# Joining two matmuls of 256 columns into one of 512 in three of the seven Strassen products of a SwiGLU gate/up pair

## The chip, the cores and the metric

The kernel runs on one core of one Trainium2 chip. The metric is device time in microseconds (us) of one execution. Differences between kernels are told against the kernel before on the same chip.

The core has five engines with a queue of instructions each: TensorE (PE, matrix products into PSUM; its weight loads are listed as PEld), VectorE (DVE), ScalarE (ACT), GpSimd (POOL), and SyncE (SP, which here only issues loads). Each engine works through its own queue in order, and waits on semaphores where an operand comes from another engine or a buffer is still in use.

## What is computed

Two layers of an encoder block on x of 512 tokens by 1024 features, in float32:

```python
for l in range(2):
    x = x + 0.5 * swiglu(rms_norm(x, ffn1_norm[l]), w_gate1[l], w_up1[l], w_down1[l])
    h = rms_norm(x, mix_norm[l])
    p = h @ w_in[l]
    ...                       # attention on one part of p, a convolution on the other
    x = x + concat([attn, conv]) @ w_out[l]
    x = x + 0.5 * swiglu(rms_norm(x, ffn2_norm[l]), w_gate2[l], w_up2[l], w_down2[l])
    x = rms_norm(x, post_norm[l])

def swiglu(x, w_gate, w_up, w_down):          # 1024 -> 2816 -> 1024
    return (silu(x @ w_gate) * (x @ w_up)) @ w_down
```

The change lies in swiglu, which runs four times (two in each layer; "FFN 1" to "FFN 4" below, in order of time).

## The kernel before

**Split operands.** A float32 operand is held as two tiles: hi, the value rounded to the type that TensorE multiplies (fp32r), and lo, the rest. ACT makes hi with a copy, DVE makes lo with a subtraction. A product is three matmuls into the same PSUM area (`mm3`, lines 151 to 155): weight hi by activation hi (L152), weight hi by activation lo (L153), weight lo by activation hi (L154).

**Chunks and pairs.** The 2816 hidden features are 11 pairs of 2 x 128 (a pair is gate and up of 256 hidden features). `CHUNKS` (line 39) groups the pairs of an FFN as (0,1), (2,3,4), (5,6,7), (8,9,10). The loop is in `ffn_body`, lines 491 to 573.

- Chunk 0 is done with plain products of 512 tokens. In its second half the generator `operands` (lines 304 to 346) makes the activation operands for all later pairs, in steps that `advance` doles out between the plain work: from four quarters of the scaled x it forms the seven Strassen operands b11, b21, b22, t1 to t4 and splits each with `halved` (lines 306 to 312), 14 times in an FFN: one ACT copy of 128x512 (L310) and one DVE subtraction of 128x512 (L311), which give one hi tile and one lo tile that each hold two 256-token blocks. Behind it comes a plain down projection of 8 blocks: for each block the weight is split (L136 on ACT, L142 on DVE), multiplied, and added to x by DVE (L558).
- Every pair of chunks 1 to 3 (`pair`, lines 377 to 428; 9 in an FFN, 36 in all) is one level of Strassen-Winograd: 7 products instead of 8, on weight quarters of 128x1024 that hold gate and up side by side. `product` (lines 348 to 357) does one of them in 24 matmuls of 256 columns: 4 blocks of k, three matmuls each, for gate and for up. Gate lies in the first, up in the second half of one PSUM bank.
- Chunks 1 and 2 end with `down` (lines 430 to 477), the down projection as Strassen products, two column groups g of seven products each; a product has 6 `mm3`, so 18 matmuls of 256 columns. Chunk 3 ends with a plain down projection.

**Order inside a pair.** The products run in the order b11, b21, t2, t3, t1, t4, b22. Accumulation is in three PSUM banks: bx takes b11, t2, t1 and b22; by takes b21; bz takes t3 and t4. Between them the partial sums are copied out by ACT (`copied`, L360) or added by DVE: L389 adds by, L400 forms the difference of bz and bx after t1, L402 adds bz after t4, L408 and L409 read bx after b22. silu is L391, L405 and L408, the product with up L392, L406 and L409. The weight sums for the next pair are four DVE additions of 128x1024 (L385 to L388), which may start only after L400 of the pair before (`order["first"]`). ACT makes the hi of a weight sum (L242, L374) and DVE its lo (L244); for b21 and t4 the lo comes through a POOL DMA that adds (`subtracted`, L366 and L367). The last pair before a `down` is followed there by L460, L461 and L465 in place of L386 to L388 (weights of 128x768), and in `down` each finished product is added into x by DVE straight from PSUM (L449), ahead of the next product that accumulates in the same bank.

**What sets the order.** The queues of the engines are not written by hand: the program is built with a scheduler that orders each engine's instructions by its own estimates, under the dependencies and the hints `tc.issue_after`. PE takes all products in program order. Weight buffers hold four hi tiles and four lo tiles (`bufs=4`), PSUM has a pool of seven banks, and short-lived tiles come from a pool of five (`tmp`).

Of the kernel before, what the change touches and what calls it, by code (L numbers as in the profile page):

```python
# [15 lines left out]
P = 128  # L16
D = 1024
S = 512
# [37 lines left out]
WOP = 4  # L56
EVP = "DAD"
ORDER = "t0s1p3v4o5"

VECS = [("g1", 8), ("gm", 8), ("g2", 8), ("gp", 8), ("gql", 3), ("gkl", 2),  # L60
        ("cw", 4 * CK), ("cb", 4), ("lg", 4), ("lb", 4), ("gq", 1), ("gk", 1)]
# [11 lines left out]
def encoder_kernel(ctx: ExitStack, tc: tile.TileContext, xT, consts, vecs, rgain, wgu1, wd1, wdq1,  # L73
# [177 lines left out]
    def ffn_body(fpool, l, gx, norm, wgu, wd, wdq, gain, done, w0, halved):  # L251
# [52 lines left out]
        def operands(R):  # L304

            def halved(src, own=False):
                hi, lo = (fpool.tile([P, S], FR, tag="xs", name=nm("xs"), bufs=2) if own else slot(FR)
                          for _ in range(2))
                h3, l3 = (v.rearrange("p (j t) -> p j t", j=2) for v in (hi, lo))
                A.copy(h3, src)  # L310
                V.tensor_tensor(l3, src, h3.bitcast(FP), ALU.subtract)  # L311
                return hi, lo

            def diff(a, b, op=ALU.subtract):
                t = tmp().rearrange("p (j t) -> p j t", j=2)
                V.tensor_tensor(t, a, b, op)
                return t
            for i in range(2):
                e, o = wide(quarter()), wide(quarter())
                for j in range(2):  # L320
                    for par, t in ((0, e), (1, o)):
                        m = 4 * i + 2 * j + par
                        V.scalar_tensor_tensor(t[:, j], x[:, m, :], gain[:, m:m + 1], R, ALU.mult, ALU.mult)
                        yield
                b11, b12, b21, b22 = (v[:, :, h * HS:(h + 1) * HS] for v in (e, o) for h in range(2))
                for n, src in (("b11", b11), ("b21", b21)):
                    X[n].append(halved(src))
# [5 lines left out]
                X["t2"].append(halved(t2))  # L333
                yield
                X["t3"].append(halved(t3))
                yield
                t1 = diff(b11, b12)
                yield
                X["t1"].append(halved(t1))
                yield  # L340
                t4 = diff(b21, t2, ALU.add)
                yield
                X["t4"].append(halved(t4))
                yield
                X["b22"].append(halved(b22, i == 1))
                yield

        def product(o, w, n, start, stop):
            with tc.issue_after(order["pe"]):
                for gu in range(2):  # L350
                    for k in range(4):
                        hi, lo = X[n][k // 2]
                        t = slice(k % 2 * HS, (k % 2 + 1) * HS)
                        c = slice(gu * 512 + k * P, gu * 512 + (k + 1) * P)
                        last = mm3(o[:, gu * HS:(gu + 1) * HS], w[0][:, c], w[1][:, c], hi[:, t], lo[:, t],
                                   start and gu == 0 and k == 0, stop and k == 3, True)
            order["pe"] = last

        def copied(o, src):
            A.copy(o, src)  # L360
            return o

        def subtracted(w, src, n=WC):

# [12 lines left out]
        def pair(p, quartered):  # L377

            a11, a12, a21, a22, s3 = quarters(wgu[l, p], WC, p == CHUNKS[0][1])
            bx, by, bz = bank(), bank(), bank()  # L380
            product(bx, split_into("a11", a11), "b11", True, True)
            a = copied(tmp(), bx)
            product(by, summed(wgu[l, p, 1], a12), "b21", True, True)
            with after("first"):
                V.tensor_tensor(s3, a11, a21, ALU.add)  # L385
                V.tensor_tensor(a21, a21, a22, ALU.add)  # L386
                V.tensor_tensor(a11, a11, a21, ALU.add)  # L387
                V.tensor_tensor(a12, a12, a11, ALU.add)  # L388
# [11 lines left out]
            order["first"] = V.tensor_tensor(r2[:, 1], d, r2[:, 1], ALU.subtract).ins  # L400
            product(bz, summed(wgu[l, p, 3], a22), "t4", False, True)
            V.tensor_tensor(r2[:, 0], bz, r2[:, 0], ALU.subtract)  # L402
# [3 lines left out]
            V.tensor_tensor(s2v, s2v, r2[:, :, HS:S], ALU.mult)  # L406
            product(bx, split_into("s4", a12), "b22", False, True)
            A.activation(s[:, HS:S], bx[:, 0:HS], AF.Silu)  # L408
            V.tensor_tensor(s[:, HS:S], s[:, HS:S], bx[:, HS:S], ALU.mult)  # L409
# [8 lines left out]
            V.tensor_tensor(u[:, h0], s[:, h1], s2[:, h1], ALU.subtract)  # L418
            order["u0"] = V.tensor_tensor(u[:, h1], u[:, h0], s[:, h0], ALU.subtract).ins
            V.tensor_tensor(v[:, h0], s[:, h0], s[:, h1], ALU.subtract)  # L420
            V.tensor_tensor(v[:, h1], s2[:, h0], u[:, h1], ALU.add)
# [785 lines left out]
```

## Time and profile before

| what | before |
|---|---|
| median of 3 runs | 1806.97 us (1805.7 to 1807.44) |
| profiled execution, span of the core | 1803.8 us |
| profiled execution, mean granted TensorE clock | 0.999 |
| matmuls on PE in the trace | 12198 |
| POOL busy | 422.2 us, 23% of the span |
| DMA moved | 226.23 MB, mean 125 GB/s |

The span runs from the first to the last instruction of the profiled execution; the profile gives no other time of that execution, and the median of the runs lies 3.2 us above the span. A row of a timeline has the start in us from the span's beginning, the duration in us, the engine, the line of the kernel, the operation, output and inputs by their names in the program, their shapes, and in brackets how long the engine had been idle before and what released it. Matmuls are pipelined: consecutive ones overlap, so what one costs is the step from its start to the next start, not its duration.

### The profile page before, as it was taken

What the parts mean: (1) busy time and instruction counts of PE and PEld (TensorE: products, weight loads), DVE (VectorE), ACT (ScalarE), POOL (GpSimd) and SP (SyncE); (2) the same over time, 40 slices, a digit from 0 to 9 for tenths busy, and PEclk for the clock granted to TensorE, in tenths of its full rate; (3) what the DMA queues carried; (4) which work ended last, traced back from release to release, by engine and by line L of the source; (5) the groups of instructions that cost most, each with busy time, mean ns of one, the idle gap of its engine ahead of it and who ended that gap; (6) DMA issues with size and microseconds to landing.
All of it is one profiled execution on the core that took longest, in us unless ns stands there. A gap on an engine that the chain in (4) does not pass through costs nothing.

```text
span 1803.8 us, 30598 instructions
## 1 busy us (share of the span) xinstructions
PE 1786.7 (99%) x12198; PEld 1645.8 (91%) x12198; DVE 1423.3 (79%) x1975; ACT 1088.8 (60%) x1685; POOL 422.2 (23%) x343
## 2 busy tenths in 40 slices
PE   9999999999999999999999999999999999999998
PEld 7899999888788899999888999998978788999997
DVE  7888887588956979887779888866999668888873
ACT  5565656457953565656635656554779535656564
POOL 1000000258843000000310000002589410000001
PEclk9999999999999999999999999999999999999999
DMA  5657574324102466664326575743250126575742
GB/s 172 165 132 193 123 187 112 108 88 135 31 24 99 126 163 162 151 163 126 123 65 170 122 195 121 194 110 110 80 147 6 52 79 167 129 189 126 187 112 73
DMA packets 70415, 226.23 MB, mean 125 GB/s; under 512 B 7936, under 2 KB 8320, under 8 KB 70272
## 3 DMA queue, kind: packets, MB, share of 16 engines
q1 hardware_dynamic: 54000, 169.74, 28.1%
q0 software_dynamic: 16128, 54.53, 17.7%
q8 instruction: 95, 1.56, 0.4%
q14 instruction: 48, 0.39, 0.1%
q10 hardware_dynamic: 144, 0.00, 0.0%
HBM read 222.15 MB, written 2.10 MB: 124 GB/s over the span
## 4 chain that ended last, share of the span: by engine, by line
PE 80%; DVE 8%; ACT 5%; POOL 3%; issue 3%; DMA 1%; SPq 0%; ACTq 0%; POOLq 0%; DVEq 0%
PE ps L154 26%; PE ps L152 25%; PE ps L153 25%; POOL y L896 2%; PE ps L834 1%; DVE wl L244 1%; ACT pr L892 1%; DVE x L449 1%; DVE r L160 1%; ACT r L806 1%; PE ps L800 1%; DVE wl L142 1%; DVE cv L888 1%; DMA raw<-in_wgu 1%; ACT wh L136 1%
## 5 line engine op out<-in xcount | busy, mean ns | idle before, releaser
L153 PE MATMUL ps<-r,wh 128*128 128x256 f32 (+1 forms) x3436 | 1062.3, 309 | 0.1
L152 PE MATMUL ps<-r,wh 128*128 128x256 f32 (+1 forms) x3436 | 1061.0, 311 | 0.6 <-ACT r L159 0.3
L154 PE MATMUL ps<-r,wl 128*128 128x256 f32 (+1 forms) x2668 | 845.6, 318 | 2.6 <-DVE wl L142 1.2
L152 PEld LDWEIGHTS ps<-r,wh 128*128 128x128 f32 x3436 | 650.9, 190 | 38.6 <-ACT wh L136 2.1
L153 PEld LDWEIGHTS ps<-r,wh 128*128 128x128 f32 x3436 | 652.3, 190 | 36.4 <-issue 2.4
L154 PEld LDWEIGHTS ps<-r,wl 128*128 128x128 f32 x2668 | 506.9, 190 | 41.3 <-DVE wl L142 3.0
L136 ACT CAST wh<-raw 128x1024 fp32r<-128x1024 f32 (+3 forms) x148 | 132.1, 900 | 211.0 <-issue 101.3
L367 POOL DMA_DIRECT2D ls<-in_wgu x72 | 62.5, 869 | 741.7 <-ACT ls L366 615.3
L242 ACT CAST wh<-fr 128x1024 fp32r<-128x1024 f32 (+1 forms) x160 | 157.6, 985 | 101.5 <-DVE fr L387 39.7
L142 DVE TENSOR_TENSOR wl<-raw,wh 128x1024 fp32r<-128x1024 f32 (+3 forms) x132 | 146.8, 1117 | 91.0 <-ACT wh L136 90.0
L154 PE MATMUL ps<-r,ls 128*128 128x256 f32 x768 | 216.7, 282 | 0.0
L244 DVE TENSOR_TENSOR wl<-fr,wh 128x1024 fp32r<-128x1024 f32 (+1 forms) x160 | 182.9, 1143 | 40.3 <-ACT wh L242 40.3
L896 POOL TENSOR_TENSOR y<-y,pr 128x511 f32<-128x511 f32 (+14 forms) x120 | 157.4, 1312 | 54.6 <-ACT pr L892 47.4
L154 PEld LDWEIGHTS ps<-r,ls 128*128 128x128 f32 x768 | 145.2, 189 | 0.0
L244 DVE TENSOR_TENSOR wl<-raw,wh 128x1024 fp32r<-128x1024 f32 (+1 forms) x100 | 113.7, 1137 | 24.6 <-ACT wh L242 24.1
L189 POOL TENSOR_TENSOR r<-r,t 128x512 f32<-128x512 f32 x45 | 77.4, 1728 | 172.7 <-ACT t L185 171.9
L242 ACT CAST wh<-raw 128x1024 fp32r<-128x1024 f32 (+1 forms) x100 | 97.9, 979 | 27.9 <-PE ps L153 19.9
L366 ACT ACTIVATE ls<-fr 128x1024 fp32r<-128x1024 f32 (+1 forms) x56 | 56.1, 1002 | 78.6 <-PE ps L154 65.2
L892 ACT ACTIVATE pr<-r,vec 128x511 f32<-128x511 f32 (+14 forms) x120 | 85.3, 735 | 10.1 <-POOL y L896 10.1
L888 DVE SCALAR_TENSOR_TENSOR cv<-r,vec,cv 128x511 f32<-128x511 f32 (+14 forms) x120 | 88.0, 733 | 3.4 <-ACT cv L884 2.1
L449 DVE SCALAR_TENSOR_TENSOR x<-ps,x 128x512 f32<-128x512 f32 x112 | 77.1, 689 | 15.8 <-PE ps L154 15.4
L367 POOL DMA_DIRECT2D ls<-in_wdq x32 | 27.6, 863 | 260.5 <-ACT ls L366 260.5
(220 smaller groups left out, 2441.5 us busy)
## 6 DMA issues: line engine op xcount, KB each, us to landing
fr<-in_wgu SPq DMA_DIRECT2D x112, 512.0 KB, 3.4
ls<-in_wgu POOLq DMA_DIRECT2D x72, 512.0 KB, 6.3
raw<-in_wgu SPq DMA_DIRECT2D x62, 512.0 KB, 5.0
fr<-in_wdq SPq DMA_DIRECT2D x48, 384.0 KB, 4.6
ls<-in_wdq POOLq DMA_DIRECT2D x32, 384.0 KB, 4.7
raw<-in_wd SPq DMA_DIRECT2D x32, 384.0 KB, 3.1
raw<-in_wd SPq DMA_DIRECT2D x32, 256.0 KB, 2.7
raw<-in_wcv SPq DMA_DIRECT2D x16, 512.0 KB, 3.2
```

The lines of the kernel that those rows point to most:

```text
L136: order["cast"] = A.copy(hi[:, :w], raw[:, :w]).ins
L142: (G if kind in POOLW.split() else V).tensor_tensor(lo[:, :w], raw[:, :w], hi[:, :w].bitcast(FP), ALU.subtract)
L152: T.matmul(o, lh, rh, start=first, stop=False, skip_group_check=free)
L153: T.matmul(o, lh, rl, start=False, stop=False, skip_group_check=free)
L154: order["mm"] = T.matmul(o, ll, rh, start=False, stop=last, skip_group_check=free).ins
L242: A.copy(hi[:, :w], src[:, :w])
L244: order["lo"] = V.tensor_tensor(lo[:, :w], src[:, :w], hi[:, :w].bitcast(FP), ALU.subtract).ins
L367: G.dma_start(out=lo[:, :n], in_=w, accum_op=ALU.add)
L449: return V.scalar_tensor_tensor(v, o.rearrange("p (m t) -> p m t", m=2), 0.5 * sign, v, ALU.mult, ALU.add).ins
L888: V.scalar_tensor_tensor(acc[:, s:], u[c][:, :S - s], tap(k), acc[:, s:], ALU.mult, ALU.add)
L892: A.activation(pr[:, s:], u[c][:, :S - s], AF.Copy, scale=tap(k))
L896: order["conv"] = G.tensor_tensor(acc[:, s:], acc[:, s:], pr[:, s:], ALU.add).ins
```

## The change

In the products b21, t4 and b22 the two matmuls that share a weight tile, hi by hi and hi by lo, become one matmul of 512 columns. For that, hi and lo of an activation block have to lie side by side, and so do the two results:

- `halved` makes, for each of the two 256-token blocks, one tile with hi in the first and lo in the second half. It issues two ACT copies and two DVE subtractions of 128x256 in place of one each of 128x512, for all seven operands.
- Each of bx, by and bz becomes two banks, one for gate and one for up (six banks in place of three). A joined product leaves hi by hi plus lo by hi in the first half of each bank (the main part), and hi by lo in the second half (the rest).
- `product` issues 16 matmuls for the three joined names (8 of 512 and 8 of 256 columns) and 24 of 256 as before for b11, t2, t3 and t1.
- `copied` is two ACT copies of 128x256. Where by and bz are read, DVE adds main and rest of both halves in four instructions of 128x256 in place of one of 128x512. After b22 both halves are first copied out by ACT into a new short-lived tile y, DVE adds the rest in two instructions, and silu and the product with up read y and no longer PSUM.

`down`, the plain products and the attention and convolution part have no edit.

```diff
+JOINED = ("b21", "t4", "b22")
...
             def halved(src, own=False):
-                hi, lo = (fpool.tile([P, S], FR, tag="xs", name=nm("xs"), bufs=2) if own else slot(FR)
-                          for _ in range(2))
-                h3, l3 = (v.rearrange("p (j t) -> p j t", j=2) for v in (hi, lo))
-                A.copy(h3, src)
-                V.tensor_tensor(l3, src, h3.bitcast(FP), ALU.subtract)
-                return hi, lo
+                made = []
+                for j in range(2):
+                    both = fpool.tile([P, S], FR, tag="xs", name=nm("xs"), bufs=2) if own else slot(FR)
+                    A.copy(both[:, 0:HS], src[:, j])
+                    V.tensor_tensor(both[:, HS:S], src[:, j], both[:, 0:HS].bitcast(FP), ALU.subtract)
+                    made.append(both)
+                return made
...
-        def product(o, w, n, start, stop):
+        def product(os, w, n, start, stop):
             with tc.issue_after(order["pe"]):
-                for gu in range(2):
+                for gu, o in enumerate(os):
                     for k in range(4):
-                        hi, lo = X[n][k // 2]
-                        t = slice(k % 2 * HS, (k % 2 + 1) * HS)
+                        both = X[n][k]
                         c = slice(gu * 512 + k * P, gu * 512 + (k + 1) * P)
-                        last = mm3(o[:, gu * HS:(gu + 1) * HS], w[0][:, c], w[1][:, c], hi[:, t], lo[:, t],
-                                   start and gu == 0 and k == 0, stop and k == 3, True)
+                        first, end = start and k == 0, stop and k == 3
+                        if n in JOINED:
+                            T.matmul(o, w[0][:, c], both, start=first, stop=False, skip_group_check=True)
+                            last = T.matmul(o[:, 0:HS], w[1][:, c], both[:, 0:HS], start=False, stop=end,
+                                            skip_group_check=True).ins
+                        else:
+                            last = mm3(o[:, 0:HS], w[0][:, c], w[1][:, c], both[:, 0:HS], both[:, HS:S],
+                                       first, end, True)
             order["pe"] = last
 
-        def copied(o, src):
-            A.copy(o, src)
+        def copied(o, os):
+            for gu in range(2):
+                A.copy(o[:, gu * HS:(gu + 1) * HS], os[gu][:, 0:HS])
             return o
+
+        def parts(os):
+            return [(slice(gu * HS, (gu + 1) * HS), o[:, 0:HS], o[:, HS:S]) for gu, o in enumerate(os)]
...
-            bx, by, bz = bank(), bank(), bank()
+            bx, by, bz = ((bank(), bank()) for _ in range(3))
...
-            V.tensor_tensor(a, a, by, ALU.add)
             s = tmp()
-            A.activation(s[:, 0:HS], a[:, 0:HS], AF.Silu)
+            for c, main, rest in parts(by):
+                V.tensor_tensor(a[:, c], a[:, c], main, ALU.add)
+                V.tensor_tensor(a[:, c], a[:, c], rest, ALU.add)
+                if c.start == 0:
+                    A.activation(s[:, 0:HS], a[:, 0:HS], AF.Silu)
...
-            V.tensor_tensor(r2[:, 0], bz, r2[:, 0], ALU.subtract)
+            for c, main, rest in parts(bz):
+                V.tensor_tensor(r2[:, 0, c], main, r2[:, 0, c], ALU.subtract)
+                V.tensor_tensor(r2[:, 0, c], rest, r2[:, 0, c], ALU.add)
...
-            A.activation(s[:, HS:S], bx[:, 0:HS], AF.Silu)
-            V.tensor_tensor(s[:, HS:S], s[:, HS:S], bx[:, HS:S], ALU.mult)
+            y = copied(tmp(), bx)
+            for c, main, rest in parts(bx):
+                V.tensor_tensor(y[:, c], y[:, c], rest, ALU.add)
+                if c.start == 0:
+                    A.activation(s[:, HS:S], y[:, c], AF.Silu)
+            V.tensor_tensor(s[:, HS:S], s[:, HS:S], y[:, HS:S], ALU.mult)
```

More of the change, by code (lines that the diff above doesn't have):

```diff
@@ L326, in operands @@
                 for n, src in (("b11", b11), ("b21", b21)):
-                    X[n].append(halved(src))
+                    X[n].extend(halved(src))
                     yield
@@ L332, in operands @@
                 yield
-                X["t2"].append(halved(t2))
+                X["t2"].extend(halved(t2))
                 yield
-                X["t3"].append(halved(t3))
+                X["t3"].extend(halved(t3))
                 yield
@@ L338, in operands @@
                 yield
-                X["t1"].append(halved(t1))
+                X["t1"].extend(halved(t1))
                 yield
@@ L342, in operands @@
                 yield
-                X["t4"].append(halved(t4))
+                X["t4"].extend(halved(t4))
                 yield
-                X["b22"].append(halved(b22, i == 1))
+                X["b22"].extend(halved(b22, i == 1))
                 yield
-        def product(o, w, n, start, stop):
+        def product(os, w, n, start, stop):
             with tc.issue_after(order["pe"]):
-                for gu in range(2):
+                for gu, o in enumerate(os):
                     for k in range(4):
-                        hi, lo = X[n][k // 2]
-                        t = slice(k % 2 * HS, (k % 2 + 1) * HS)
+                        both = X[n][k]
                         c = slice(gu * 512 + k * P, gu * 512 + (k + 1) * P)
-                        last = mm3(o[:, gu * HS:(gu + 1) * HS], w[0][:, c], w[1][:, c], hi[:, t], lo[:, t],
-                                   start and gu == 0 and k == 0, stop and k == 3, True)
+                        first, end = start and k == 0, stop and k == 3
[6 more added lines that the diff above has]
+                                       first, end, True)
             order["pe"] = last
-        def copied(o, src):
-            A.copy(o, src)
-            return o
+        def copied(o, os):
+            for gu in range(2):
+                A.copy(o[:, gu * HS:(gu + 1) * HS], os[gu][:, 0:HS])
+            return o
+        def parts(os):
+            return [(slice(gu * HS, (gu + 1) * HS), o[:, 0:HS], o[:, HS:S]) for gu, o in enumerate(os)]
         def subtracted(w, src, n=WC):
```

## The prediction

> **What bounds the kernel now.** I read the page first, then the busy time by window in one steady pair, then TensorE's and VectorE's timelines where products meet.
>
> ```profile
> span 1803.8 us, 30598 instructions
> ...
> PE 1786.7 (99%) x12198; PEld 1645.8 (91%) x12198; DVE 1423.3 (79%) x1975; ACT 1088.8 (60%) x1685; POOL 422.2 (23%) x343
> ...
> PE 80%; DVE 8%; ACT 5%; POOL 3%; issue 3%; DMA 1%; SPq 0%; ACTq 0%; POOLq 0%; DVEq 0%
> ```
>
> ```profile
> 94.59:114.65 20.06, 20.06 (x171) 20.06 (x169) 17.04 (x24) 14.27 (x20) 1.73 (x2) 1.00 0.60 145
> ```
>
> TensorE is busy 99% of the span and 80% of the chain that ended last. The second fence is one pair of chunk 1, from one first product to the next: 20.06 us, PE without a gap (its clock 1.00), DVE busy 17.04 us, ACT 14.27. So a step on PE that gets shorter counts in full, as long as DVE keeps up, and DVE has 3.0 us to spare in 20.
>
> ```profile
> 65.93 0.39 PE L152 MATMUL ps<-r,wh 128*128 128x512 f32 x1
> ...
> 74.09 0.39 PE L153 MATMUL ps<-r,wh 128*128 128x512 f32 x1
> ...
> 108.95 0.28 PE L152 MATMUL ps<-r,wh 128*128 128x256 f32 x1
> ...
> 111.79 0.28 PE L152 MATMUL ps<-r,wh 128*128 128x256 f32 x1
> ...
> 114.65 0.28 PE L152 MATMUL ps<-r,wh 128*128 128x256 f32 x1
> ...
> 143.31 0.29 PE L152 MATMUL ps<-r,wh 128*128 128x256 f32 x1
> 143.43 0.28 PE L153 MATMUL ps<-r,wh 128*128 128x256 f32 x1
> ```
>
> **Part 1, the joins.** From 65.93 to 74.09 lie 36 steps of 512 columns, 0.2267 us each. The product t4 runs from 108.95 to 111.79 and b22 from there to 114.65: 24 steps of 256 columns each, 0.1183 and 0.1192 us. The joined product has 8 steps of 512 and 8 of 256: 8 x (0.2267 + 0.119) = 2.77 us in place of 2.84 (t4, and b21, which has the same weights' path) or 2.86 (b22). The saving is 0.07 + 0.07 + 0.09 = 0.23 us in a pair; if the joined product's 256-column steps keep 0.1183 and its 512-column ones are a nanosecond shorter it is 0.28. I take 0.25 x 36 pairs = **-9.0 us**, with 8 and 11.5 as ends (8: 0.23 x 36; 11.5: 864 joins, which are 3 products x 8 x 36, at twice the 0.12 from 143.31 to 143.43, less 0.2267).
>
> The Trainium skill, "TensorE: Matmul & The Clock Gate", section "Back-to-back issue gap", speaks against the join: a matmul steps by its columns at 2.4 GHz plus about 2.5 ns, and by that (my estimate from the page) a join gains only those 2.5 ns, 2.2 us in 864. The rows above have 118 to 119 ns where that formula has 109, and 227 where it has 216, so each matmul here carries some 12 ns beside its columns, and the trace does not bear the page out.
>
> **Part 2, inside a pair.** The prices of DVE's steps are from the place behind the last pair, where it works without a pause:
>
> ```profile
> 136.55 0.43 DVE L418 TENSOR_TENSOR u<-t,t 128x256 f32<-128x256 f32 x1
> 136.89 0.42 DVE L420 TENSOR_TENSOR t<-t 128x256 f32<-128x256 f32 x1
> 137.23 0.42 DVE L419 TENSOR_TENSOR u<-u,t 128x256 f32<-128x256 f32 x1
> 137.56 0.68 DVE L449 SCALAR_TENSOR_TENSOR x<-ps,x 128x512 f32<-128x512 f32 x1
> 138.16 0.41 DVE L421 TENSOR_TENSOR t<-t,u 128x256 f32<-128x256 f32 x1
> ```
>
> From L418 to L420 a 256-column DVE step takes 0.34 us, from L449 to L421 a 512-column one 0.60. DVE gets three more instructions at by, three at bz and two at bx, all 128x256; ACT gets six copies of 256 in place of, or beside, 512. So by and bz cost 4 x 0.34 - 0.60 = 0.76 each and bx 0.68: DVE gets 2.2 us more in a pair, 19.2 of some 19.8. It still fits, barely. What must be on time is the lo half of the weight sum for the next pair's t2:
>
> ```profile
> 110.65 0.69 DVE L400 TENSOR_TENSOR e<-t,e 128x512 f32<-128x512 f32 x1 [1.81 <-ACT e L360]
> ...
> 118.60 1.23 DVE L244 TENSOR_TENSOR wl<-fr,wh 128x1024 fp32r<-128x1024 f32 x1
> ...
> 120.60 0.28 PE L154 MATMUL ps<-r,wl 128*128 128x256 f32 x1
> ```
>
> L244 ends at 119.83, the first matmul that reads it starts at 120.60: 0.77 us of cover. In the order in which the changed program is built, the four weight sums stay interleaved with the small adds, the splitting of silu's result moves behind L244, and the work from L400 to L244's start is 8.1 us (before: 118.60 - 110.65 = 7.95). It starts about 0.2 earlier, since the copy before it is half as long; PE arrives 0.25 earlier. Cover left: about 0.5 us, cost **0**. If that cover is gone, each of the 24 pair-to-pair steps pays what is missing. The six banks of seven cost nothing: in the built order a new pair's banks are those of by and bz of the pair before, read a product or more earlier.
>
> **Part 3, from the last pair of a chunk into `down`** (8 times). Here the weight sums are short and the DVE queue holds the update of x that `down`'s third product waits for.
>
> ```profile
> 130.49 0.69 DVE L400 TENSOR_TENSOR e<-t,e 128x512 f32<-128x512 f32 x1 [2.08 <-ACT e L360]
> 131.10 0.95 DVE L460 TENSOR_TENSOR fr<-fr,fr 128x768 f32<-128x768 f32 x1
> 132.04 0.69 DVE L402 TENSOR_TENSOR e<-ps,e 128x512 f32<-128x512 f32 x1
> 132.65 0.95 DVE L461 TENSOR_TENSOR fr<-fr,fr 128x768 f32<-128x768 f32 x1
> 133.52 0.68 DVE L406 TENSOR_TENSOR t<-t,e 128x512 f32<-128x512 f32 x1
> 134.56 0.96 DVE L244 TENSOR_TENSOR wl<-fr,wh 128x768 fp32r<-128x768 f32 x1 [0.36 <-ACT wh L242]
> 135.44 0.68 DVE L160 TENSOR_TENSOR r<-t,r 128x512 fp32r<-128x512 f32 x1
> 136.09 0.42 DVE L409 TENSOR_TENSOR t<-t,ps 128x256 f32<-128x256 f32 x1
> ```
>
> ```profile
> 129.00 0.28 PE L152 MATMUL ps<-r,wh 128*128 128x256 f32 x1
> ...
> 138.99 0.28 PE L152 MATMUL ps<-r,wh 128*128 128x256 f32 x1
> ...
> 143.83 0.38 PE L154 MATMUL ps<-r,wl 128*128 128x256 f32 x1
> 144.05 0.28 PE L152 MATMUL ps<-r,wh 128*128 128x256 f32 x1
> ```
>
> ```profile
> 133.69 0.84 ACT L242 CAST wh<-fr 128x768 fp32r<-128x768 f32 x1 [0.28 <-DVE fr L461]
> 134.43 0.61 ACT L159 CAST r<-t 128x512 fp32r<-128x512 f32 x1
> ```
>
> Count from T, the start of t4 (129.00). Before, L449 ran from T+8.56 to T+9.25, and t2 of `down`, which accumulates in the bank that L449 reads, started at T+9.99: 0.7 us of cover. In the changed program's built order L449 stands behind L400 0.61, L460 0.94, L461 0.87, the four adds of bz and the lo of b11's activation 5 x 0.34, a wait, L244 0.88, a wait, L406 0.60, the two adds of bx 0.68, a wait, L160 0.60, L409 to L419 1.47. The waits: L244 waits for its ACT cast, which starts at L461's end + 0.09 and lasts 0.84; L406 now waits for silu (L405), which the new order of ACT's queue puts behind that cast and a second one of the same size; L160 for its own ACT copy of 0.61, which can only follow L406. From T+1.3 on: L461 ends at 4.8, the cast at 5.7, L244 gives way at 6.6, the second cast at 6.35, silu (0.63) ends at 6.98, L406 runs to 7.6, the adds of bx to 8.3, L160 8.4 to 9.0, the rest to 10.5, L449 to 11.15. PE wants t2 at 9.99 less the 0.16 gained: 9.83. It stands for **1.4 us**, and some 0.2 more at t1, whose bank's update slips likewise. In return the stop at 143.43 (0.40 to the next step and 0.22 to the one after, against 0.12 each: 0.38 us) goes, since t1's lo is now early enough. Net 1.2 x 8 = **+9.6 us**; ends: 0.6 a time if silu is not held by the casts (4.8), 1.6 if the small adds cost 0.42 and not 0.34 (13).
>
> **Part 4, chunk 0** (4 times). The 14 halvings become 28 on each engine: 14 x (0.68 - 0.60) = 1.1 us more on DVE. What matters is the order: PE waits for the weight half of the fourth plain down block (L142).
>
> ```profile
> 61.75 1.29 DVE L558 SCALAR_TENSOR_TENSOR x<-ps,x 128x512 f32<-128x512 f32 x2 [0.65 <-PE ps L154]
> 62.95 0.68 DVE L311 TENSOR_TENSOR r<-t,r 128x512 fp32r<-128x512 f32 x1
> 63.55 0.69 DVE L558 SCALAR_TENSOR_TENSOR x<-ps,x 128x512 f32<-128x512 f32 x1
> 64.15 0.68 DVE L142 TENSOR_TENSOR wl<-raw,wh 128x512 fp32r<-128x512 f32 x1
> ```
>
> ```profile
> 64.89 0.50 PE L154 MATMUL ps<-r,wl 128*128 128x512 f32 x1 [0.27 <-DVE wl L142]
> ```
>
> ```profile
> 613.65 0.68 DVE L142 TENSOR_TENSOR wl<-raw,wh 128x512 fp32r<-128x512 f32 x1
> ```
>
> The first update L558 waits for PE, so it cannot start before 61.75; then came two updates, one halving, one update and L142, whose end at 64.83 released the matmul at 64.89. In the built order of the changed program four updates and seven small halvings stand between 61.75 and L142's end: 4 x 0.60 + 7 x 0.34 + 0.69 = 5.5 us, 67.2: PE stands 2.35 us longer. FFN 2 (613.65) and FFN 4 have the same order before and after: 3 x 2.35. In FFN 3 all halvings stood ahead of L142 already; I take 0 (ends -0.4 and +1.3, the latter the 1.1 us of DVE time and a little waiting). Sum **+7.0 us**, ends 3 and 9. Attention, convolution and the plain parts keep the order of every queue that I compared, and cost 0; the loads of the pairs' weights wait for buffers that are freed within a microsecond of before, against several microseconds of lead.
>
> The Trainium skill, "VectorE: DVE Perf Modes", section on the TRN2 errata, gives the same durations as these rows, 424 and 691 ns by its formula, and advises tiles of 512 or more; on its durations alone a split would cost 157 ns and the halvings 2.2 us, an estimate. The starts above overlap, which makes it 0.08.
>
> **The sum:** 1803.8 - 9.0 + 9.6 + 7.0 = 1811.4 us of span. The median of the runs is 3.2 above the span, so **1814.6 us**.
>
> **The rivals.**
> - *Only PE counts:* the covers hold in `down` and in chunk 0. For it: DVE has 3.0 us of 20 to spare on average. Against: the two stops at 64.89 and 143.83 show that in just these places DVE has none. 1807.0 - 9.0 = 1798.0. Chance 0.08; this one is faster.
> - *One of parts 3 and 4 is hidden:* 1805.0 (without 3) or 1807.6 (without 4). Chance 0.18; within 0.2% of now.
> - *DVE becomes the bound of every pair* (the slow side): the 0.5 us of cover before t2 goes, because the small PSUM adds cost 0.42 instead of 0.34, or wait for ACT between each other. It decides once the work from L400 to L244 exceeds 8.6 us. With 0.5 us missing at 24 pair ends, 12 us more: 1826.6. Chance 0.18.
> - *The join gains next to nothing on PE*, each matmul's cost being its columns: 2.2 in place of 9.0 us, 1821.4 with parts 3 and 4. Chance 0.05; the rule of "TensorE: Matmul & The Clock Gate" above would have it so. Joined products of 2.84 us would show it.
>
> **How the numbers follow.** Forecast 0.51, the rivals as given; 0.2% (3.6 us) is about what a measurement of this kernel can tell from no change. The forecast's own ends, 1806 to 1821, put 0.07 of its chance within 0.2%. Faster: 0.08 and a little of the second rival, 0.10. Same: 0.16 + 0.07 = 0.23. Slower: 0.44 + 0.18 + 0.05 = 0.67. The range leaves out the first rival and the upper half of the third: 1802 to 1825.
>
> **What would show it.** Part 1: b21, t4 and b22 at 2.77 us each. Part 2: no gap on PE at a pair's t2. Part 3: PE idle 1 to 1.5 us at the third product of the first column group, released by L449's line, and no idle at t1's lo. Part 4: about 3 us of idle on PE in the plain down of chunk 0 in FFN 1, 2 and 4, released by the weight split. Gaps inside the pairs would prove me wrong on the slow side, none in `down` on the fast side.

## The result, and the profile after

The changed kernel takes 1817.25 us (median of 5 runs, 1816.99 to 1818.89); the kernel before takes 1806.97. The ratio is 1.0062, 95% interval 1.005 to 1.0074. That is 10.3 us more by the medians and 11 by the ratio, where 7.6 more were forecast (1814.6; range 1802 to 1825).

The page of the changed kernel, its line of spans, of busy time, of engines in the chain, and three of its groups of instructions (busy us and mean ns; then idle time before them and what ended most of it):

```profile
span 1817.1 us, 29627 instructions
...
PE 1785.0 (98%) x11334; PEld 1604.4 (88%) x11334; DVE 1500.4 (83%) x2319; ACT 1131.7 (62%) x1957; POOL 420.4 (23%) x343
...
PE 82%; DVE 7%; ACT 5%; issue 3%; POOL 3%; DMA 1%; ACTq 0%; SPq 0%; POOLq 0%; DVEq 0%
...
L153 PE MATMUL ps<-r,wh 128*128 128x256 f32 (+1 forms) x2716 | 859.1, 320 | 13.2 <-DVE x L470 9.7
...
L155 PE MATMUL ps<-r,wl 128*128 128x256 f32 (+1 forms) x2524 | 801.5, 320 | 6.0 <-DVE wl L143 5.5
...
L358 PE MATMUL ps<-r,wh 128*128 128x512 f32 x720 | 255.3, 394 | 0.0
```

PE has 864 matmuls fewer, as 864 joins must give, and its busy time fell by only 1.7 us (from 1786.7). DVE has 344 instructions and 77 us more. Two releasers stand out: the update of x in `down` (L470, before L449), 9.7 us, and the weight's lo half in chunk 0 (L143, before L142), 5.5 us. The same two and the next in the view of waits, whose columns are the instruction and what it waited for, us in total, times, and the longest:

```profile
PE ps L153 <- DVE x L470: 9.7, 8, 1.2
PE ps L155 <- DVE wl L143: 5.5, 4, 1.9
PE ps L153 <- ACT wh L137: 2.5, 3, 1.3
```

In the same view of the kernel before, the update isn't listed at all and the weight half has this row:

```profile
PE ps L154 <- DVE wl L142: 1.2, 4, 0.4
```

PE's order is the same in both kernels but for the joins and a few exchanged neighbours, so each matmul of one trace can be laid beside its counterpart in the other, and the difference of their starts read at the ends of the stages. What each stage adds to it:

| stage | us, profile after less before |
|---|---|
| 36 pairs | -7.0 |
| eight times from the last pair into `down` | +11.2 (1.36 to 1.41 each) |
| chunk 0 of FFN 1, 2, 3, 4 | +2.7, +4.1, -0.4, +2.1 |
| program start, and all else | +0.6 |
| sum | +13.3 (1817.1 less 1803.8) |

The medians differ by 10.3, 3 us less than the profiled executions. The profiled execution of the changed kernel took 1818.9 us, the longest of its five runs and 1.6 above their median; by its trace 1.6 us of FFN 2's +4.1 have a cause of their own, told last. A run of it takes 1.8 us more than its span (1818.9 and 1817.1); by the same step the profiled execution of the kernel before, with its span of 1803.8, is the run of 1805.7, the shortest of its runs and 1.3 below their median.

**The joins.** Matmuls of one pair in PE's timeline: the first two of b21 (L358 is a joined matmul, L359 the product with the weight's lo), and the first and third of t2 behind it:

```profile
120.19 0.39 PE L358 MATMUL ps<-r,wh 128*128 128x512 f32 x1
120.42 0.28 PE L359 MATMUL ps<-r,ls 128*128 128x256 f32 x1
...
122.97 0.28 PE L153 MATMUL ps<-r,wh 128*128 128x256 f32 x1
...
123.21 0.28 PE L155 MATMUL ps<-r,wl 128*128 128x256 f32 x1
```

From 120.19 to 122.97 the joined product takes 2.78 us; over all pairs the mean steps are 0.232 us for 512 columns and 0.116 for 256. The pair falls from 20.05 to 19.85 us. No gap on PE lies in it, and its row by window (PE, PEld, DVE, ACT, POOL busy, then clock) shows DVE at 18.97 of 19.85 us (it is at 19.24 in the last pair of the chunk):

```profile
97.50:117.35 19.85, 19.85 (x147) 18.81 (x146) 18.97 (x32) 15.18 (x26) 1.73 (x2) 1.00 0.62 147
```

The lo half of the weight sum that t2's third matmul (123.21) reads ends at 122.53, 0.68 us ahead:

```profile
121.31 1.22 DVE L245 TENSOR_TENSOR wl<-fr,wh 128x1024 fp32r<-128x1024 f32 x1
```

**Into `down`.** DVE, and then PE, in the first of the eight places:

```profile
137.26 0.96 DVE L245 TENSOR_TENSOR wl<-fr,wh 128x768 fp32r<-128x768 f32 x1 [0.29 <-ACT wh L243]
138.72 0.69 DVE L423 TENSOR_TENSOR t<-t,e 128x512 f32<-128x512 f32 x1 [0.50 <-ACT t L422]
...
142.17 0.68 DVE L470 SCALAR_TENSOR_TENSOR x<-ps,x 128x512 f32<-128x512 f32 x1
```

```profile
131.60 0.39 PE L358 MATMUL ps<-r,wh 128*128 128x512 f32 x1
...
139.32 0.28 PE L153 MATMUL ps<-r,wh 128*128 128x256 f32 x1
...
142.91 0.39 PE L153 MATMUL ps<-r,wh 128*128 128x256 f32 x1 [1.21 <-DVE x L470]
```

t4 starts at T = 131.60. The update ends at T+11.25 (before: T+9.25); a product of `down` takes 2.13 us, so the third could have started that long after the second (139.32), at T+9.85, and starts at T+11.31.

**Chunk 0.** PE waits twice in FFN 1, first for the weight's hi (L137 on ACT), then for its lo; DVE's rows say why the second comes late:

```profile
64.70 0.50 PE L153 MATMUL ps<-r,wh 128*128 128x512 f32 x1 [1.30 <-ACT wh L137]
...
67.94 0.50 PE L155 MATMUL ps<-r,wl 128*128 128x512 f32 x1 [1.46 <-DVE wl L143]
```

```profile
62.47 0.68 DVE L579 SCALAR_TENSOR_TENSOR x<-ps,x 128x512 f32<-128x512 f32 x1
...
66.20 1.08 DVE L312 TENSOR_TENSOR r<-t,r 128x256 fp32r<-128x256 f32 x3
67.20 1.88 DVE L143 TENSOR_TENSOR wl<-raw,wh 128x512 fp32r<-128x512 f32 x3
```

Between 62.47 and 67.20 lie the four updates and seven small halvings of the built order.

### The profile page after: what moved, and what is told of

It reads as the page before. It is cut to its first block, busy times and chain, and to the rows that moved or that the text cites. A ratio compares the mean times of both kernels' runs of the same rounds, so it can differ in the third digit from the quotient of the medians.

```text
span 1817.1 us, 29627 instructions
## 1 busy us (share of the span) xinstructions
PE 1785.0 (98%) x11334; PEld 1604.4 (88%) x11334; DVE 1500.4 (83%) x2319; ACT 1131.7 (62%) x1957; POOL 420.4 (23%) x343
## 4 chain that ended last, share of the span: by engine, by line
PE 82%; DVE 7%; ACT 5%; issue 3%; POOL 3%; DMA 1%; ACTq 0%; SPq 0%; POOLq 0%; DVEq 0%
PE ps L153 20%; PE ps L155 20%; PE ps L154 20%; PE ps L358 11%; PE ps L359 6%; POOL y L917 2%; PE ps L855 1%; PE ps L821 1%; ACT pr L913 1%; DMA fr<-in_wgu 1%; DVE r L312 1%; DVE wl L143 1%; DVE cv L909 1%; DVE fr L325 1%; ACT r L827 1%
## 5 line engine op out<-in xcount | busy, mean ns | idle before, releaser
L153 PE MATMUL ps<-r,wh 128*128 128x256 f32 (+1 forms) x2716 | 859.1, 320 | 13.2 <-DVE x L470 9.7
L154 PE MATMUL ps<-r,wh 128*128 128x256 f32 (+1 forms) x2716 | 860.9, 317 | 0.0
L155 PE MATMUL ps<-r,wl 128*128 128x256 f32 (+1 forms) x2524 | 801.5, 320 | 6.0 <-DVE wl L143 5.5
L153 PEld LDWEIGHTS ps<-r,wh 128*128 128x128 f32 x2716 | 515.5, 190 | 58.6 <-DVE x L470 11.3
L154 PEld LDWEIGHTS ps<-r,wh 128*128 128x128 f32 x2716 | 515.9, 190 | 36.1 <-issue 2.4
L155 PEld LDWEIGHTS ps<-r,wl 128*128 128x128 f32 x2524 | 478.3, 190 | 42.9 <-DVE wl L143 7.2
L358 PE MATMUL ps<-r,wh 128*128 128x512 f32 x720 | 255.3, 394 | 0.0
L137 ACT CAST wh<-raw 128x1024 fp32r<-128x1024 f32 (+3 forms) x148 | 131.5, 900 | 191.0 <-PE ps L154 110.9
L143 DVE TENSOR_TENSOR wl<-raw,wh 128x1024 fp32r<-128x1024 f32 (+3 forms) x132 | 145.7, 1115 | 80.4 <-ACT wh L137 79.8
L245 DVE TENSOR_TENSOR wl<-fr,wh 128x1024 fp32r<-128x1024 f32 (+1 forms) x160 | 182.2, 1139 | 33.6 <-ACT wh L243 33.6
L359 PE MATMUL ps<-r,ls 128*128 128x256 f32 x576 | 160.2, 278 | 0.0
L358 PEld LDWEIGHTS ps<-r,wh 128*128 128x128 f32 x720 | 135.4, 188 | 27.8
L245 DVE TENSOR_TENSOR wl<-raw,wh 128x1024 fp32r<-128x1024 f32 (+1 forms) x100 | 113.3, 1133 | 11.1 <-ACT wh L243 10.7
L378 ACT ACTIVATE ls<-fr 128x1024 fp32r<-128x1024 f32 (+1 forms) x56 | 56.1, 1001 | 85.3 <-PE ps L359 48.1
L359 PEld LDWEIGHTS ps<-r,ls 128*128 128x128 f32 x576 | 108.5, 188 | 0.0
L368 ACT COPY t<-ps 128x256 f32<-128x256 f32 x216 | 76.2, 368 | 28.4 <-PE ps L359 19.5
```

Of the source, the lines that this page charges most:

```text
L137: order["cast"] = A.copy(hi[:, :w], raw[:, :w]).ins
L143: (G if kind in POOLW.split() else V).tensor_tensor(lo[:, :w], raw[:, :w], hi[:, :w].bitcast(FP), ALU.subtract)
L153: T.matmul(o, lh, rh, start=first, stop=False, skip_group_check=free)
L154: T.matmul(o, lh, rl, start=False, stop=False, skip_group_check=free)
L155: order["mm"] = T.matmul(o, ll, rh, start=False, stop=last, skip_group_check=free).ins
L245: order["lo"] = V.tensor_tensor(lo[:, :w], src[:, :w], hi[:, :w].bitcast(FP), ALU.subtract).ins
```

## The experiments

All are compared with the kernel before on the same chip, with 95% intervals of the ratio. The theory at first: each loss is one instruction that stands too late in a queue (the update in `down`, the weight half in chunk 0). The rivals: the added DVE work is paid wherever it stands; six banks in place of three cost something.

**1. The halvings alone** (kernel before, edited).

```diff
-                A.copy(h3, src)
-                V.tensor_tensor(l3, src, h3.bitcast(FP), ALU.subtract)
+                for j in range(2):
+                    A.copy(h3[:, j], src[:, j])
+                    V.tensor_tensor(l3[:, j], src[:, j], h3[:, j].bitcast(FP), ALU.subtract)
```

> The kernel before, with one part of the change alone: each of the 14 halvings of chunk 0 is two ACT copies and two DVE subtractions of 128x256. Theory (one late instruction in a queue): in the built order four updates and two small halvings stand ahead of the weight half of the fourth plain down block in FFN 1, 2 and 4, 4 x 0.60 + 2 x 0.34 = 3.1 us, where before had 2.4; so three stops longer by 0.7 us, about +2 us, 1809. Rival (the added DVE work itself is paid): 14 x 0.08 = 1.1 us in each of four FFNs, +4.5, 1811.5. Rival (splitting the halvings is what costs the 6.8 us that chunk 0 lost): 1814.

1810.09 us, ratio 1.0019 (1.001 to 1.0028). The stops at the weight half, all in FFN 1, 2 and 4:

```profile
PE ps L154 <- DVE wl L142: 4.4, 3, 1.5
```

By the trace, whose span is 4.9 us longer, FFN 1, 2 and 4 stand 1.0 to 1.1 us longer each at this stop, and FFN 3 no longer by anything clear. The largest other piece, 1.7 us, lies behind the attention and convolution of the second layer, where nothing is edited: PE comes back there from a pause (at 1405.2), and four of its steps of 512 columns take 0.427 us each. The time alone does not part +2 from +4.5; that the loss in the edited part sits in three stops and not in four FFNs does speak for the order. The split as such does not cost chunk 0's 7 us: the order that it led to in the changed kernel does (run 2).

**2. The order in chunk 0** (changed kernel, one hint).

```diff
                 if p0 == 0:
-                    advance(2)
+                    with tc.issue_after(order["cast"]):
+                        advance(2)
```

> The changed kernel, with one hint: the halvings that run beside the plain down of chunk 0 are ordered, on ACT, behind the newest cast of a down weight. The work is the same. In the built order two or three updates and one halving stand ahead of the weight half of the fourth block, not four updates and seven halvings. Theory (order): the stops of 2.9 us in FFN 1, 2 and 4 fall to 0.7 or less; -6.8 us, ratio to before near 1.002. Rival (DVE's added work): nothing is taken away, so within 1 us of the changed kernel, ratio near 1.006.

1810.46 us, ratio 1.0024 (1.0015 to 1.0034): 6.9 us less than the changed kernel (1.0062), with the same work. The weight half and the matmul that waited for it, now:

```profile
63.65 0.69 DVE L143 TENSOR_TENSOR wl<-raw,wh 128x512 fp32r<-128x512 f32 x1
```

```profile
64.39 0.50 PE L155 MATMUL ps<-r,wl 128*128 128x512 f32 x1
```

67.94 became 64.39. For chunk 0 the theory holds and the rival falls.

**3. The update placed earlier** (changed kernel, one hint taken away).

```diff
-                with after("u0"):
-                    add(0, 0, px, 1)
+                add(0, 0, px, 1)
```

> The changed kernel without the hint that holds the first update of x in down behind the difference u. In the built order the update then stands right behind the product with silu, seven small instructions and a split earlier. Theory (the update is late in DVE's queue): the stop of 1.4 us at down's third product goes, and u's own split comes 0.9 us later, which gives 0.2 to 0.8 us back at down's fourth and fifth product; -6 to -10 us, ratio 1.0005 to 1.003. Rival (DVE's added work): the same work in another order, the stop only moves to the next product; within 2 us of the changed kernel. Rival (the six banks are read late): the same as the theory for the first stop, so this run does not tell it from the theory.

1824.55 us, ratio 1.0101 (1.0087 to 1.0115): 7 us more than the changed kernel, not 6 to 10 less. The update did move, and PE no longer waits for it:

```profile
141.18 0.69 DVE L470 SCALAR_TENSOR_TENSOR x<-ps,x 128x512 f32<-128x512 f32 x1
...
142.44 0.68 DVE L161 TENSOR_TENSOR r<-t,r 128x512 fp32r<-128x512 f32 x1
...
145.46 0.69 DVE L161 TENSOR_TENSOR r<-u,r 128x512 fp32r<-128x512 f32 x1 [0.41 <-ACT r L160]
```

```profile
PE ps L154 <- DVE r L161: 6.8, 16, 0.5
```

But the two splits behind it are now late: the lo of silu's second result, which the second product reads, and the lo of u, which the fourth reads; 16 waits, two in each `down`, and a third for L245. By the matmul-by-matmul comparison `down` costs 16.8 us, not 11.2. So for `down` the theory falls in its first form: a row of DVE results is due there one after the other, and bringing one forward makes the next late. What counts is how much stands in DVE's queue ahead of all of them.

**4. No joins of t4 and b22 before `down`** (changed kernel; the additions of their rest are left out there, where nothing is in it).

```diff
+            joined = () if quartered else JOINED
...
-                V.tensor_tensor(r2[:, 0, c], rest, r2[:, 0, c], ALU.add)
+                if not quartered:
+                    V.tensor_tensor(r2[:, 0, c], rest, r2[:, 0, c], ALU.add)
...
-                V.tensor_tensor(y[:, c], y[:, c], rest, ALU.add)
+                if not quartered:
+                    V.tensor_tensor(y[:, c], y[:, c], rest, ALU.add)
```

> The changed kernel, but in the last pair before each down t4 and b22 are not joined, and the additions of the rest of bz and bx are left out there (nothing is in it); b21 stays joined, all six banks and the split halvings stay. Theory (small additions and silu behind two casts put the update late): the eight stops fall from 1.6 to before's 0.4 us, 8 x 0.16 us of joins are lost; -8 us, ratio near 1.0015. Rival (six banks): the banks are as in the changed kernel, the stops stay, +1.3 us, ratio near 1.007.

1811.02 us, ratio 1.0028 (1.0018 to 1.0038). `quartered` holds in all three pairs of chunks 1 and 2, so 24 pairs lost two joins, not eight; that is why it is 2 us above the expectation. By stage: pairs -4.0 (not -7.0), `down` +2.2 (not +11.2), chunk 0 as in the changed kernel. The update is gone from the list of waits with all six banks in place, so the rival of the six banks falls.

**5. The layout alone, and 6. joins without the additions.** Run 5 has `JOINED = ()` and no rest to add; run 6 keeps the joins and leaves out the six additions of the rest, so hi times lo of three products is missing from its output. They have the same instructions on DVE, ACT and POOL, in the same order but for a few places (25 of 2103 on DVE, 21 of 1957 on ACT).

```diff
-                V.tensor_tensor(a[:, c], a[:, c], rest, ALU.add)
...
-                V.tensor_tensor(r2[:, 0, c], rest, r2[:, 0, c], ALU.add)
...
-                V.tensor_tensor(y[:, c], y[:, c], rest, ALU.add)
```

> The changed kernel with no product joined, and without the additions of the rest (nothing is in it); the layout stays: six banks, 256-column copies, split halvings. Theory (chunk 0 pays 6.8 us for its order, down pays for the small additions of the rest, and the joins earn 0.20 us a pair): nothing is earned, down's stops are near before's 0.4 us, so before + 6.8 + about 1, ratio 1.004. Rival (layout and six banks cost in every pair or in down): 1.3 us more in each of eight downs, ratio near 1.009.

> The changed kernel with its joins, but the six additions of the rest in a pair are left out (the output lacks hi times lo of the three products). DVE, ACT and POOL have the same queues as in the kernel with the layout alone, so the difference of the two is what the joins earn on PE: 36 x 0.20 = 7.2 us by the changed kernel's trace. Theory: ratio near 1.000 (chunk 0 still pays 6.8, the joins give 7.2). Rival (joins earn next to nothing): the same time as the layout alone. Against the changed kernel it gives the price of the small additions: theory 8 x 1.3 = 10.4 us, all of it in down.

1816.10 us, ratio 1.0055 (1.0043 to 1.0068), and 1808.98, ratio 1.0018 (1.0009 to 1.0027): the joins earn 7.1 us, as the theory has it, not next to nothing. Both stand some 3 us above what was expected. By stage run 5's pairs take the time of the kernel before (0.03 us apart at most, the first of an FFN left out) and its `down` 0.8 us more in all eight, so the layout with its six banks costs next to nothing in either. Run 6 has +1.4 in `down` in place of +11.2 (the additions' price is 9.8 us, and it is paid there), -7.0 in the pairs and +8.8 in chunk 0. So 2 us of the 3 are chunk 0, where FFN 2 met a slow clock again (0.54 from 617.5 to 621.2 us), and 1.4 are in `down`, where a weight half comes late in the second column group:

```profile
PE ps L155 <- DVE wl L245: 1.8, 6, 0.3
```

**7. Silu ahead of a cast** (changed kernel).

```diff
-                with after("u"):
+                with after("u"), after("silu"):
                     times(pz, s3, "t3", True)
```

(`order["silu"]` is L422.)

> The changed kernel with one hint: ACT's cast of t3's weights in down comes behind silu of the last pair (L422), not before it; DVE's order is the same. Theory (silu waits behind a cast, and everything on DVE up to the update of x waits for silu): silu starts 0.9 us earlier, DVE's idle of 0.50 us ahead of the product with silu goes, the update is 0.35 to 0.6 us earlier, the stop falls from 1.4 to about 0.9; -3 to -4.5 us, ratio near 1.004. Rival (the small additions alone fill DVE): no change, ratio near 1.006.

1816.52 us, ratio 1.0061 (1.0048 to 1.0074): no change. Silu did come earlier (137.20 instead of 138.06), and so did the product and the update:

```profile
138.20 0.68 DVE L423 TENSOR_TENSOR t<-t,e 128x512 f32<-128x512 f32 x1
...
141.72 0.68 DVE L470 SCALAR_TENSOR_TENSOR x<-ps,x 128x512 f32<-128x512 f32 x1
142.32 0.41 DVE L442 TENSOR_TENSOR t<-t,u 128x256 f32<-128x256 f32 x1
143.11 0.69 DVE L161 TENSOR_TENSOR r<-u,r 128x512 fp32r<-128x512 f32 x1 [0.38 <-ACT r L160]
```

The wait for the update shrank by 3.2 us over the eight places, but u's lo still came at 143.11 (143.12 in the changed kernel), since its hi copy on ACT (L160) stands behind the negated weight copy (L378), which waits for PE; `down` costs 10.5 us in place of 11.2. The wait for silu is real and is not what decides.

**8. Both remedies** (changed kernel with run 2's hint, and run 4's edit in the one pair before each `down` alone).

```diff
-            joined = () if quartered else JOINED
+            joined = () if quartered and p + 1 in [c1 for _, c1 in CHUNKS] else JOINED
```

> The changed kernel with two edits: the hint that put the down weight of chunk 0 ahead of the halvings, and t4 and b22 not joined in the one pair before each down (their rest additions left out there; nothing is in them). Theory: chunk 0 gives back 6.8 us, down 8 x 1.3, less 8 x 0.12 of joins: 1817.25 - 6.8 - 10.4 + 1.0 = 1801, ratio 0.997, faster than before. Rival (the added DVE work is paid somewhere in any case, as the run with the update placed earlier let one think): the gains do not add, ratio 1.000 or above.

1800.29 us, ratio 0.9967 (0.9956 to 0.9977): below both kernels, and within 1 us of the expectation. By stage: pairs -5.3, `down` +1.7, chunk 0 -1.9, all else +0.6: -4.9 in the profile. DVE at the first place, with PE's third product behind:

```profile
133.44 0.69 DVE L425 TENSOR_TENSOR t<-t,e 128x512 f32<-128x512 f32 x1
...
137.95 0.68 DVE L473 SCALAR_TENSOR_TENSOR x<-ps,x 128x512 f32<-128x512 f32 x1
```

```profile
138.68 0.28 PE L155 MATMUL ps<-r,ls 128*128 128x256 f32 x1
138.80 0.28 PE L153 MATMUL ps<-r,wh 128*128 128x256 f32 x1
```

The update ends at 138.63, 0.17 us ahead of the matmul that needs it.

**9. The hint without the joins** (kernel before with run 2's hint).

> The kernel before, with the hint alone that puts the down weight of chunk 0 ahead of the halvings. Theory: before stops there for 0.73, 0.73, 1.07 and 0.73 us, and in the built order one halving fewer stands ahead of the weight half; -1 to -2 us, ratio 0.999 to 0.9995, so that the joins, and not the hint, make the kernel with the plain last pair 5 us faster than before. Rival (the hint is worth 6.8 us in any kernel): ratio 0.996.

1803.95 us, ratio 0.9991 (0.9982 to 1.0): worth 1.6 us there, at the edge of what the interval can tell from nothing. Against 0.9967 the joins with the plain last pair earn some 4 us of their own.

**10. DVE work added inside the pairs** (changed kernel).

```diff
                 V.tensor_tensor(r2[:, 0, c], rest, r2[:, 0, c], ALU.add)
+                if p + 1 not in [c1 for _, c1 in CHUNKS]:
+                    V.tensor_tensor(r2[:, 0, c], rest, r2[:, 0, c], ALU.add)
+                    V.tensor_tensor(r2[:, 0, c], r2[:, 0, c], rest, ALU.subtract)
```

> The changed kernel with four more DVE instructions of 128x256 (the rest of bz added once more and subtracted again) in each of the 24 pairs that another pair follows. In the changed kernel DVE is busy 18.97 of the 19.85 us of a pair, so 0.88 us are free; four steps of 0.334 are 1.34. Theory (DVE is a hair from being the bound of each pair): PE must wait 0.46 us in each, 24 x 0.46 = +11 us on the changed kernel, 1828, ratio 1.012; up to 1.015 where the instructions stand ahead of the weight sum. Rival (DVE's slack inside the pairs is larger than its idle time shows, because the order is rebuilt): within 3 us of the changed kernel, ratio 1.006 to 1.008.

1896.17 us, ratio 1.0496 (1.0482 to 1.0511): 78 us more than the changed kernel, far beyond both. The waits, the window of the first stop, and the window behind it:

```profile
PE ps L153 <- ACT t L368: 48.1, 16, 3.1
```

```profile
103.00:106.20 3.20, 0.24 (x2) 0.00 (x0) 3.20 (x6) 3.18 (x6) 0.69 (x1) 1.00 0.73 201
106.20:110.50 4.30, 4.14 (x22) 4.15 (x23) 4.27 (x12) 2.20 (x6) 0.18 (x1) 0.61 0.78 181
```

The 16 stops (all in chunks 1 and 2) are at t2 of a pair that follows another, and not for the weight half that the prediction watched: the bank bx is read late. In the stop DVE and ACT both work without a pause (3.20 and 3.18 of 3.20 us). In the second such place DVE has silu's product (L426) behind two weight halves, ACT's copy for its split (L160) needs it and stands behind a weight copy, and the copy of b11's result (L368) stands behind these in ACT's queue:

```profile
129.63 0.60 ACT L160 CAST r<-t 128x512 fp32r<-128x512 f32 x1
130.14 0.41 ACT L432 ACTIVATE t<-t 128x256 f32<-128x256 f32 x1
130.46 0.62 ACT L368 COPY t<-ps 128x256 f32<-128x256 f32 x2
```

So DVE is indeed a hair from being the bound in chunks 1 and 2: with the additions it is busy 20.7 to 21.2 us in a pair of 23.2 to 24.7 (FFN 1), where the changed kernel's pair takes 19.85. In chunk 3 the same additions cost nothing; there DVE goes from 16.78 to 18.16 us in the second pair. Crossing the bound costs a stop of 3.0 us each time (48.1 in 16), not the missing half microsecond, and behind 15 of the 16 stops PE's steps are slower for a while, some 26 us in all by these steps: together 74 of the 78 us.

**11. Only t4 plain, and 12. only b22 plain** (both on run 8).

```diff
-            product(bx, split_into("s4", a12), "b22", False, True, joined)
+            product(bx, split_into("s4", a12), "b22", False, True)
```

(run 11, with the rest of bx added in every pair; run 12 has the same edit at t4, with bz.)

> The kernel with the hint and the plain last pair, but there b22 is joined again (its two additions of the rest are back), t4 stays plain. In the kernel with both plain the update ends 0.17 us ahead of down's third product. Theory (each small addition ahead of the update counts in full): 2 x 0.33 - 0.17 = 0.5 us of stop in each down, less 0.07 of the join: +3.5 us on that kernel, 1804, ratio 0.9986. Rival (DVE waits there for ACT anyway, so two additions are hidden): 1800 or a little less, ratio 0.9965.

> The kernel with the hint and the plain last pair, but there t4 is joined again (the two additions of the rest of bz are back, ahead of silu), b22 stays plain. In the built order ACT then puts the weight cast ahead of silu again and DVE the lo of the weight ahead of the product. Theory (additions and the wait for silu both count): 2 x 0.33 and up to 0.5 us of wait, less 0.17: 0.5 to 1.0 us of stop in each down, +3.5 to +7.5 on that kernel, ratio 0.9986 to 1.001. Rival (only the additions behind silu count): ratio 0.9965.

1809.24 us, ratio 1.0019 (1.001 to 1.0028), and 1806.08, ratio 1.0001 (0.9992 to 1.001): 9 and 5.8 us above run 8; by stage 9.0 and 5.4 of it are in `down`. Run 12 is as expected in size: PE is 0.9 us later at each third product, 0.6 of it already in the second, where the lo of silu's second result comes late. In run 11 a stop of 0.5 us was expected at each third product, and PE is 0.3 later there; a further 1.2 us behind it were not expected: u's hi copy fell behind L378 on ACT, which waits for PE,

```profile
138.48 0.85 ACT L378 ACTIVATE ls<-raw 128x768 fp32r<-128x768 f32 x1 [2.45 <-PE ps L155]
139.23 0.60 ACT L160 CAST r<-u 128x512 fp32r<-128x512 f32 x1
```

```profile
139.87 0.69 DVE L161 TENSOR_TENSOR r<-u,r 128x512 fp32r<-128x512 f32 x1 [1.03 <-ACT r L160]
```

and DVE stood for 1.03 us ahead of u's lo. In run 8 the two were the other way round on ACT. So even two small additions ahead of `down` count in full, and through the order that the scheduler makes of them for more than that.

## Why the prediction was right

- **Sign and mechanism held.** Joins earn, `down` and chunk 0 lose more: -7.0, +11.2 and, without the slow clock, +6.9 against -9.0, +9.6 and +7.0. The errors of the first two have the same sign and add to 3.6 us; that the medians are only 2.7 above the forecast's 7.6 comes in part from the profile of the kernel before, a run 1.3 below its median.
- **Part 1 was sized too high, by 2 us.** The working took the plain product's 0.2267 us for a joined step and 0.119 for the rest; in the joined product they are 0.232 and 0.116, so a pair gains 0.20 us, not 0.25. Runs 5 and 6 differ by 7.1 us. By the formula of the Trainium skill, "TensorE: Matmul & The Clock Gate", section "Back-to-back issue gap", which it calls the gap of a single, isolated matmul, 864 joins would earn 2.2 us, an estimate; the measurement decides against it here.
- **Part 2 was right in its sum, and incomplete.** No pair stops; DVE is at 18.97 to 19.24 of 19.85 in the fullest pairs (forecast 19.2 of 19.8), and the weight half ends 0.7 us ahead of t2. What it missed is a second cover, ACT's copy of b11's bank, which run 10 used up first.
- **Part 3 was right in its place and within 0.2 us in its size.** Update's end T+11.25 (forecast 11.15), t2 wanted at T+9.85 (9.83), stop 1.4 (1.4). Net 1.4 a time, not 1.2: t1's 0.2 came as forecast, and before's 0.38 us went, but restarting costs about 0.1 us more at each stop. Its lower end, 0.6 a time if silu is not held by the casts, was wrong: run 7 freed silu and `down` still cost 1.3. The additions are the cause (runs 4, 6 and 8), and not through the update alone (run 3).
- **Part 4 was right in size and in its three FFNs,** +2.7, +2.5 (4.1 less the 1.6 below), -0.4 and +2.1 against 3 x 2.35 and 0. A third of the stops is ACT's cast (L137, 2.5 of 8.0 us of waits), behind eight small copies, which the working did not name.
- **The rivals.** That DVE becomes the bound of every pair did not happen, but run 10 shows that its price was taken much too low (0.5 us a pair, where a stop took 3.0). That the joins gain next to nothing is excluded by runs 5 and 6, that six banks cost by runs 4 and 5.

## What to carry to other kernels

A saving on the bound engine has to be read against the place where its helper's queue has the least slack, not against the helper's mean load: before the change DVE had 3 us of 20 to spare in a pair, and its update of x only 0.7 us on the way into `down`. Where a cheaper form costs work on the helper, use it everywhere but there: eight pairs of 36 without two joins, and one hint, turned +10 us into -5. And do not mend one late instruction before looking at what stands behind it; where several results are due in a row, moving one forward only changes which is late.

## What was not expected of the hardware

After a stop of a few microseconds PE can come back at a lower clock. In FFN 2's chunk 0 (window: PE busy time first; the clock is the third number from the end):

```profile
616.00:620.60 4.60, 2.64 (x10) 1.27 (x8) 4.60 (x12) 2.36 (x6) 0.00 (x0) 1.00 1.02 300
620.60:624.80 4.20, 3.77 (x10) 2.98 (x11) 4.17 (x6) 1.68 (x2) 0.86 (x1) 0.61 0.64 166
...
1516.00:1521.00 5.00, 2.61 (x10) 1.56 (x10) 5.00 (x12) 1.77 (x4) 0.00 (x0) 1.00 0.87 278
```

2 us of idle in 4.6 us were followed by 4.2 us at a clock of 0.61, in most of which 512-column steps took 0.427 us instead of 0.227: 1.6 us more. A like stop in FFN 4 (the third row) had no such effect: behind it, from 1521 to 1525, the clock was 1.00. Run 10 has the same 0.61 behind the first of its 16 stops of 2.9 to 3.1 us, and slower steps behind all of them but one (at 207.29): 1.0 to 2.6 us each. So a stop of 3 us cost on the mean about half as much again in this run. The Trainium skill, "TensorE: Matmul & The Clock Gate", section "Part 1: The HAM clock gate (the "warmup" mystery)", has a clock of one half after an idle window of about 3.4 us that runs free of the program; half speed and the dependence on chance agree with these rows. Here a stop of 1.9 us, with one of 0.5 and 1.8 us of work ahead of it, was enough.
